# Hybrid decoder layer, down projection: activation loads for the next chunk kept behind a pair's sums on GpSimd's queue

## The chip, the cores and the metric

One core of one Trainium2 chip runs the whole layer in one launch. The metric is the device time of an execution in microseconds (us), and of several runs the median. TensorE is the engine of the matmuls (PE in the profile, PEld for its weight loads); VectorE is DVE, ScalarE is ACT, GpSimd is POOL, SyncE is SP. SyncE and GpSimd issue the DMA transfers.

## The reference, cut to what matters

The layer adds 16 meta tokens, runs two groups of heads and a projection, and ends with a SwiGLU feed-forward part on 512 tokens, a width of 2048 and an inner width of 5632:

```python
n2 = _rmsnorm(h, g_ffn[l])
h = h + (jax.nn.silu(n2 @ w_gate[l]) * (n2 @ w_up[l])) @ w_down[l]
return h[:, N_META:]
```

The change lies in the last product, `... @ w_down`, the down projection. All is float32.

## The kernel before, in words

Every float32 product is made of three products of a faster type: weights and activations are split into a rounded part and a remainder ("hi" and "lo"), and TensorE adds hi x hi, hi x lo and lo x hi. That is why matmuls stand in threes, lines 700 to 702 of `block_product`.

The feed-forward products use a scheme for 2 x 2 blocks with seven products in place of eight. For a pair of output tiles there are four weight blocks, "11", "12", "21" and "22", and seven products, each of a sum of weight blocks with a sum of activation blocks. `pair_product` (line 704) issues the seven products of a pair in PSUM banks x, y and z: x with block 0, z with 1, x with 2, z with 3, x with 4, y with 5, and x with 6. Between them ScalarE and VectorE take sums out: line 731 reads z, line 735 reads x after block 4, and only then may block 6 be added in x; line 738 reads y. With six inner tiles to a block, one block is 18 matmuls, and a pair 126.

**The weight side.** `prepare_pair` (line 627) makes the seven split weights of a pair, somewhat ahead of their use. `split_quad` (lines 604 to 609) copies a block to hi on ScalarE (line 607) and takes the remainder on VectorE (line 608). `add_quads` (line 611, the sum itself at line 614) makes t1 = "11" + "12" and t3 = "12" + "22"; lines 648 and 621 make t2. Each of the four weight blocks has one buffer, so the next pair's block is loaded by SyncE (`load_quad`, line 589) right after the last use of this pair's block: "12" after t3, "11" after its split, "22" after its split, "21" after its last sum. In the order that the scheduler chose, t3 of the next pair, which needs the new "22", stands on VectorE directly ahead of line 735 of the current pair.

**The activation side.** The 44 inner tiles are cut in four chunks, `CHUNKS = (4, 6, 6, 6)`, counted in pairs of tiles. The seven sums of activation blocks of each chunk lie in DRAM (`fd[c][s]`, chunk c, block s), hi and lo as two parts of 768 KB each (n = 6). `load_acts(c, s)` (line 919) brings one block back into SBUF with two DMAs on GpSimd's queue (line 930 in the profile). There are twelve places for blocks (`ring_place`), a chunk uses seven, so five blocks of the next chunk may come early, and two (5 and 6) can only come when the chunk's last pair has begun to free places.

**The loops.** Chunk 0 is run for four steps of four output tiles each (lines 982 to 997), chunks 1 to 3 for eight pairs of two output tiles each (line 998 on). After each pair, `down` (line 964) multiplies by the row scale (lines 967 and 974), and `add_down` (line 959) has GpSimd issue a DMA that adds the pair's sums to the output in DRAM, one for the odd tile (behind line 967), one for the even tile (behind the second product of line 974). In the last chunk the last pair is added on the chip instead (`so_far`, loaded at line 1010).

In the program's text the loads for the next chunk stand at the head of pairs 1 to 5 (blocks 0 to 4) and at the end of pair 7 (blocks 5 and 6). That isn't the order on the queue: a scheduler places each engine's instructions by when it believes them ready, and the loads depend on little, so they move ahead of the adds that wait for VectorE. In the built program the two parts of block 0 stand around the adds of the pair before, and all five blocks are issued over about two pairs.

Of the kernel before, what the change touches and what calls it, by code (L numbers as in the profile page):

```python
# [33 lines left out]
def hybrid_layer(ctx: ExitStack, tc: tile.TileContext, xT, w_in, w_out, w_gu, w_down, vecs, out):  # L34
# [10 lines left out]
    ve, sc, gp, pe = nc.vector, nc.scalar, nc.gpsimd, nc.tensor  # L45

    def open_pool(name, bufs=1, **kw):
        return tc.alloc_tile_pool(name=name, bufs=bufs, reuse_waits="tile", **kw)
# [251 lines left out]
    def two(t):  # L300
        return t.rearrange("p (a b) -> p a b", a=2)
# [402 lines left out]
    def pair_product(acts, c1, c2, fourth=None):  # L704

        i, cols = (used[0] - WIDE) // 7, c1.shape[-1]

        def bank(name):
            return xyz.tile([P, 512], F32, tag=name, name=f"{name}{i}")[:, :cols]

        def side(name):
            n = {"p1": 0, "p5": 1, "u2": 2}[name]
            if cols == T2 or not n:
                return sides[:, n * T2 : n * T2 + cols]
            return c2[:, 2 - n]

        y, z, x = bank("y"), bank("z"), bank("x")  # L720
        p1, p5, u2 = side("p1"), side("p5"), side("u2")
        if not i:
            block_product(y, acts[5], True)
        block_product(x, acts[0], True)
        sc.copy(p1, x)
        block_product(z, acts[1], True)
        sc.copy(p5, z)  # L727
        block_product(x, acts[2], False)
        sc.copy(u2, x)
        block_product(z, acts[3], False)  # L730
        ve.scalar_tensor_tensor(c2[:, 0], z, -1.0, u2, ALU.mult, ALU.subtract)
        if fourth:
            fourth()
        block_product(x, acts[4], False)
        ve.scalar_tensor_tensor(c2[:, 1], x, -1.0, p5, ALU.mult, ALU.subtract)  # L735
        if i:
            block_product(y, acts[5], True)
        ve.tensor_tensor(c1[:, 0], y, p1, ALU.add)
        block_product(x, acts[6], False)
        return x  # L740
# [9 lines left out]
    def slots(pool, dt, m, n, name, **kw):  # L750

        c = 2 * m * n * T2
        t = pool.tile([P, c + 64], dt, name=name, **kw)
        t = t[:, 4 : 4 + c].rearrange("p (s a k t) -> p s a k t", s=m, a=2, k=n)
        return [t[:, s] for s in range(m)]

    def slot(pool, dt, n, tag, name):
        return slots(pool, dt, 1, n, name, tag=tag)[0]

    def pad(pool, n):  # L760
        pool.tile([P, n // 4], F32, name=f"pad_{pool.name}")
# [19 lines left out]
    for i, j in enumerate(OUT_TILES):  # L781
# [32 lines left out]
        if i == KT - 1:  # L814
# [10 lines left out]
            rings, n_ring, ring = {}, [6], {}  # L825
# [3 lines left out]
            def new_places(i):  # L829
                p, m = groups[i]  # L830
                for n, t in enumerate(slots(rings_p[p], F32R, m, 6, f"ring{i}", tag=f"ring{i}")):
                    ring[i + n] = t

            def ring_place():
                n_ring[0] += 1
                return ring[(n_ring[0] - 1) % 12]
# [45 lines left out]
    fd = [[dram.tile([P, 2, n, T2], F32R, name=f"fd{c}_{s}") for s in range(7)] for c, n in enumerate(CHUNKS)]  # L882
# [33 lines left out]
            ve.scalar_tensor_tensor(odd[:, 4], odd[:, 3], -1.0, odd[:, 0], ALU.mult, ALU.subtract)  # L916
            store_acts(odd, 5, (5, 6, 1, 2, 3), f // 2)

    def load_acts(c, s):
        if c < len(CHUNKS):  # L920
            n = CHUNKS[c]
            if c:
                rings[c, s] = ring_place()[:, :, :n]
            elif s:
                rings[c, s] = slot(first, F32R, n, f"first{s}", f"first{s}")
            else:
                rings[c, s] = ring[0][:, :, :n]

            for part in range(2):
                gp.dma_start(rings[c, s][:, part], fd[c][s][:, part], max_dma_last_dim=3072)  # L930

    for f in range(FT):
        g1 = apool.tile([P, 2, T2], F32, tag="c1", name=f"g{f}")
        u1 = apool.tile([P, 2, T2], F32, tag="c2", name=f"u{f}")
        x = pair_product(acts, g1, u1, None if f else h_scale)
        if f < FT - 1:
            gate(f, g1, u1, x)
        if f == 2 * CHUNKS[0] + 1:
            load_acts(0, 0)
# [4 lines left out]
    with tc.high_priority(1 << 20):  # L944
        for s in range(1, 7):
            load_acts(0, s)
# [11 lines left out]
    def add_down(j, c):  # L958
        gp.dma_start(two(out[j]), c, accum_op=ALU.add)

    def part(c, n):
        return c[:, :, n * T2 : (n + 1) * T2]

    def down(c1, c2, acts, j, so_far):

        x = pair_product(acts, c1, c2)
        ve.tensor_tensor(c2, c2, r_h, ALU.mult)
        if so_far:
            ve.tensor_tensor(c2, c2, so_far[1], ALU.add)
            nc.sync.dma_start(two(out[2 * j + 1]), c2)  # L970
        else:
            add_down(2 * j + 1, c2)
        for k, src in enumerate((c1[:, 0], x)):
            ve.tensor_tensor(c1[:, k], src, r_h[:, k], ALU.mult)
            if so_far:
                ve.tensor_tensor(c1[:, k], c1[:, k], so_far[0][:, k], ALU.add)
        if so_far:
            nc.sync.dma_start(two(out[2 * j]), c1)
        else:
            add_down(2 * j, c1)  # L980

    for j in range(KT // 4):
        for s in range(2 * j - 2, 2 * j) if j else ():
            load_acts(1, s)
        c1, c2 = ((d, d_first)[j % 2][:, m : m + 2] for m in (0, 2))
        x = pair_product([rings[0, s] for s in range(7)], c1, c2)
        if j == KT // 4 - 1:
            first.release()
            rings_p[1] = open_pool("ring_a", side="right")
            for i in (1, 3, 4, 5):  # L990
                new_places(i)
            pad(rings_p[1], 160)
            load_acts(1, 6)
        sc.copy(c1[:, 1], x)
        for m, c in ((1, c2), (0, c1)):
            for n in range(2):
                add_down(4 * j + 2 * n + m, part(c, n))
    for c in range(1, len(CHUNKS)):
        for j in range(KT // 2):

            if 1 <= j <= 5:
                load_acts(c + 1, j - 1)
            c1, c2 = (two(d[:, j % 2 * 2 + m]) for m in range(2))
            so_far = None
            if c == len(CHUNKS) - 1 and j == KT // 2 - 1:

                hh = slots(rings_p[1], F32, 1, 6, "hh", tag="ring4")[0]
                so_far = [hh[:, :, n] for n in range(2)]
                for n in range(2):
                    gp.dma_start(so_far[n], two(out[2 * j + n]))  # L1010
            down(c1, c2, [rings[c, s] for s in range(7)], j, so_far)
            if j == KT // 2 - 1:
                for s in (5, 6):
                    load_acts(c + 1, s)
# [61 lines left out]
```

## Time and profile before

| | |
|---|---|
| median of 3 runs | 2087.51 us (2087.22 to 2088.33) |
| profiled execution | 2083.55 us |
| its span, first to last instruction | 2081.8 us |
| TensorE busy | 2056.5 us, 99% |
| VectorE, ScalarE, GpSimd busy | 1634.6, 1014.7, 389.2 us |
| mean granted TensorE clock | 0.997 |
| moved by DMA | 330.40 MB, mean 159 GB/s |

In the rows of the profile, "out<-in" names what an instruction writes and reads by the program's names, without buffer numbers; "idle before" is the time in which the engine had nothing to run just before the row, and what follows the arrow is what ended it. Matmuls overlap: one takes some 275 ns, but they follow each other by 0.11 to 0.12 us in the down projection. A DMA's "time to landing" runs from its issue to its completion.

The down projection runs from about 1645 us to the end. The adds to the output are `out_T<-d` (line 959), the blocks `ring<-fd` (line 930), the weights `b<-w_down` (line 589).

### The profile page before, as it was taken

How to read it: one execution, taken by the hardware profiler on the slowest of the kernel's cores; microseconds unless marked ns; L12 is line 12 of the kernel's file. 1: busy time of each engine (PE TensorE's matmuls, PEld its weight loads, DVE VectorE, ACT ScalarE, POOL GpSimd, SP SyncE). 2: the span in 40 equal slices, each digit the busy share in tenths (PEclk: the TensorE clock that was granted, in tenths of full speed). 3: DMA queues.
4: the chain of work that ended last, by engine and by line, in shares of the span. 5: the costliest groups of instructions: out<-in, count | busy, mean ns of one | idle time of the engine just before them, and what ended most of it. 6: DMA issues, size and time to landing. Idle time of an engine off the chain costs nothing.

```text
span 2081.8 us, 39149 instructions
## 1 busy us (share of the span) xinstructions
PE 2056.5 (99%) x16086; PEld 1982.3 (95%) x16086; DVE 1634.6 (79%) x2126; ACT 1014.7 (49%) x1516; POOL 389.2 (19%) x512
## 2 busy tenths in 40 slices
PE   8999999999999999999999999999999999999999
PEld 7999999999998888999999999999999999999999
DVE  8777767533336769999898899888988978888888
ACT  6666666322223434555555555555555554444443
POOL 4111111010103444111111011011111243131210
PEclk9999999999999999999999999999999999999999
DMA  5222222232235657546555465455455999697765
GB/s 175 81 72 80 73 82 72 85 97 92 92 103 169 183 178 237 160 138 194 162 152 170 146 182 150 146 172 168 137 173 158 284 336 340 148 332 163 206 149 109
DMA packets 144115, 330.40 MB, mean 159 GB/s; under 512 B 12400, under 2 KB 62064, under 8 KB 143936
## 3 DMA queue, kind: packets, MB, share of 16 engines
q1 hardware_dynamic: 67456, 212.50, 32.1%
q0 software_dynamic: 76480, 115.40, 21.7%
q8 instruction: 126, 2.06, 0.4%
q14 instruction: 53, 0.43, 0.1%
HBM read 260.74 MB, written 67.11 MB: 157 GB/s over the span
## 4 chain that ended last, share of the span: by engine, by line
PE 93%; DVE 4%; DMA 2%; ACT 1%; issue 1%; SPq 0%; DVEq 0%; ACTq 0%
PE x L700 11%; PE x L702 11%; PE x L701 11%; PE z L700 5%; PE z L701 5%; PE z L702 5%; PE y L700 3%; PE y L702 3%; PE y L701 3%; PE po L681 3%; PE po L679 3%; PE po L680 3%; PE pv L169 2%; PE pu L173 1%; PE pc L173 1%; PE pu L169 1%
## 5 line engine op out<-in xcount | busy, mean ns | idle before, releaser
L607 ACT CAST s<-t 128x1024 fp32r<-128x1024 f32 (+1 forms) x288 | 283.2, 983 | 371.6 <-PE z L702 165.2
L608 DVE TENSOR_TENSOR s<-t,s 128x1024 fp32r<-128x1024 f32 (+1 forms) x288 | 326.7, 1134 | 102.5 <-ACT s L607 100.5
L702 PE MATMUL x<-f,s 128*128 128x256 f32 x1408 | 387.3, 275 | 1.7 <-DVE s L608 1.7
L701 PE MATMUL x<-f,s 128*128 128x256 f32 x1408 | 387.3, 275 | 1.3 <-DVE f L184 1.3
L700 PE MATMUL x<-f,s 128*128 128x256 f32 x1408 | 387.2, 275 | 0.2 <-ACT f L183 0.2
L607 ACT CAST s<-b 128x1024 fp32r<-128x1024 f32 (+1 forms) x216 | 212.4, 983 | 159.3 <-PE x L702 140.3
L702 PEld LDWEIGHTS x<-f,s 128*128 128x128 f32 x1408 | 264.3, 188 | 1.9 <-DVE s L608 1.9
L701 PEld LDWEIGHTS x<-f,s 128*128 128x128 f32 x1408 | 264.3, 188 | 1.5 <-DVE f L184 1.5
L700 PEld LDWEIGHTS x<-f,s 128*128 128x128 f32 x1408 | 264.3, 188 | 0.5 <-ACT f L183 0.4
L608 DVE TENSOR_TENSOR s<-b,s 128x1024 fp32r<-128x1024 f32 (+1 forms) x216 | 246.3, 1140 | 2.4 <-ACT s L607 1.7
L138 DVE TENSOR_TENSOR wlo<-raw,whi 128x512 fp32r<-128x512 f32 (+1 forms) x198 | 142.3, 720 | 130.9 <-ACT whi L137 130.3
L892 POOL DMA_DIRECT2D fd<-s x147 | 103.8, 927 | 690.1 <-DVE s L184 673.6
L137 ACT CAST whi<-raw 128x512 fp32r<-128x512 f32 (+1 forms) x198 | 121.3, 614 | 185.4 <-PE pu L171 65.5
L700 PE MATMUL z<-f,s 128*128 128x256 f32 x704 | 193.8, 275 | 0.7 <-ACT sides L727 0.7
L701 PE MATMUL z<-f,s 128*128 128x256 f32 x704 | 193.6, 275 | 0.0
L702 PE MATMUL z<-f,s 128*128 128x256 f32 x704 | 193.6, 275 | 0.0
L614 DVE TENSOR_TENSOR t<-b,b 128x1024 f32<-128x1024 f32 (+1 forms) x144 | 165.8, 1152 | 17.3 <-DMA b<-w_down 12.7
L700 PE MATMUL x<-ring,s 128*128 128x256 f32 x608 | 169.3, 278 | 6.7 <-DVE d L735 5.7
L702 PE MATMUL x<-ring,s 128*128 128x256 f32 x608 | 168.9, 278 | 0.5 <-DVE s L608 0.5
L701 PE MATMUL x<-ring,s 128*128 128x256 f32 x608 | 168.7, 278 | 0.0
L700 PEld LDWEIGHTS z<-f,s 128*128 128x128 f32 x704 | 132.1, 188 | 0.9 <-ACT sides L727 0.9
L702 PEld LDWEIGHTS z<-f,s 128*128 128x128 f32 x704 | 132.1, 188 | 0.0
(351 smaller groups left out, 5602.4 us busy)
## 6 DMA issues: line engine op xcount, KB each, us to landing
b<-w_gu SPq DMA_DIRECT2D x176, 512.0 KB, 3.9
raw<-w_in SPq DMA_DIRECT2D x92, 512.0 KB, 3.3
fd<-s POOLq DMA_DIRECT2D x147, 256.0 KB, 5.4
b<-w_down SPq DMA_DIRECT2D x96, 384.0 KB, 4.1
ring<-fd POOLq DMA_DIRECT2D x42, 768.0 KB, 14.7
wide<-w_out SPq DMA_DIRECT2D x30, 512.0 KB, 3.5
out_T<-d POOLq DMA_DIRECT2D x54, 256.0 KB, 4.7
b<-w_down SPq DMA_DIRECT2D x16, 512.0 KB, 7.7
```

The source lines that it names most:

```text
L137: sc.copy(hi[:, :c], raw)
L138: ve.tensor_tensor(lo[:, :c], raw, hi[:, :c].bitcast(F32), ALU.subtract)
L169: pe.matmul(ps, wh, ah[:, a:b], start=k == 0, stop=False)
L607: sc.copy(hi, src)
L608: ve.tensor_tensor(lo, src, hi.bitcast(F32), ALU.subtract)
L614: ve.tensor_tensor(sums[name], a, b, ALU.add)
L679: pe.matmul(ps, hi[:, kk], ah, start=k == 0, stop=False)
L680: pe.matmul(ps, hi[:, kk], al, start=False, stop=False)
L700: pe.matmul(p, hi[:, kk], act[:, 0, k], start=start and j == k == 0, stop=False, skip_group_check=skip)
L701: pe.matmul(p, hi[:, kk], act[:, 1, k], start=False, stop=False, skip_group_check=skip)
L702: pe.matmul(p, lo[:, kk], act[:, 0, k], start=False, stop=k == n - 1, skip_group_check=skip)
L892: gp.dma_start(fd[c][s][:, :, k], t[:, :, i])
```

## The change

`load_acts` gets an argument. Where it is set, each of the two loads is tied behind the instruction that was recorded last on GpSimd before it, by an order of issue alone: no semaphore, no waiting for the earlier one to finish. It is set for the loads at the head of pairs 1 to 5 of a chunk and for those in chunk 0's loop, not for blocks 5 and 6 (line 1014), nor for block 6 of chunk 1 (line 993), nor for chunk 0's own blocks.

```diff
-    def load_acts(c, s):
+    def load_acts(c, s, in_order=False):
...
             for part in range(2):
-                gp.dma_start(rings[c, s][:, part], fd[c][s][:, part], max_dma_last_dim=3072)
+                load = gp.dma_start(rings[c, s][:, part], fd[c][s][:, part], max_dma_last_dim=3072)
+                if in_order:
+                    tc.keep_in_program_order(load)
...
     for j in range(KT // 4):
         for s in range(2 * j - 2, 2 * j) if j else ():
-            load_acts(1, s)
+            load_acts(1, s, True)
...
             if 1 <= j <= 5:
-                load_acts(c + 1, j - 1)
+                load_acts(c + 1, j - 1, True)
```

In the built program the other engines' order is unchanged. On GpSimd the order of the down projection becomes, with "adds" for the two adds of a pair (four in chunk 0's steps):

```
chunk 0:  adds, blocks 0 1 | adds, blocks 2 3 | adds, blocks 4 5 6 | adds
chunk 1:  adds, block 0 | adds, block 1 | adds, block 2 | adds, block 3 | adds, block 4 | adds | adds, blocks 5 6 | adds
chunk 2:  adds, block 0 | adds, block 1 | adds, block 2 | adds, block 3 | adds, block 4 | adds | adds, blocks 5 6 | adds
chunk 3:  adds, with the two loads of line 1010 around the first pair's
```

Before, blocks 5 and 6 had the same place; block 0's first part stood right behind them, and the rest of blocks 0 to 4 around the adds of the next two pairs.

## The prediction

> **What bounds the kernel now.** I read the page first (busy shares, DMA issues), then who TensorE waits for in the down projection, then the timelines and the chain of waits around those waits. All names are the program's; the line numbers are those of the kernel before.
>
> ```profile
> PE 2056.5 (99%) x16086; PEld 1982.3 (95%) x16086; DVE 1634.6 (79%) x2126; ACT 1014.7 (49%) x1516; POOL 389.2 (19%) x512
> b<-w_down SPq DMA_DIRECT2D x96, 384.0 KB, 4.1
> ring<-fd POOLq DMA_DIRECT2D x42, 768.0 KB, 14.7
> ```
>
> TensorE (PE) is busy 99% of the span, so the end moves only by what TensorE idles, or by time in which its matmuls run slower. The change touches only the loads in the last row (two parts to a block) and what stands beside them on GpSimd's queue. So the question is where TensorE waits because of them. In the chunks during which they move, TensorE's timeline shows five waits:
>
> ```profile
> 1751.00 0.36 PE L700 MATMUL x<-ring,s 128*128 128x256 f32 x1 [0.56 <-DVE d L735]
> 1766.74 0.36 PE L700 MATMUL x<-ring,s 128*128 128x256 f32 x1 [1.18 <-DVE d L735]
> 1840.24 0.36 PE L700 MATMUL x<-ring,s 128*128 128x256 f32 x1 [1.85 <-DVE d L735]
> 1871.66 0.36 PE L700 MATMUL x<-ring,s 128*128 128x256 f32 x1 [0.96 <-ACT s L607]
> 1959.73 0.36 PE L700 MATMUL x<-ring,s 128*128 128x256 f32 x1 [2.11 <-DVE d L735]
> ```
>
> VectorE is named in four of them, but the chain of waits shows what held VectorE up (start, length, what):
>
> ```profile
> 1831.17 7.53 DMA b<-w_down
> ...
> 1838.80 0.96 DVE t L614
> ...
> 1840.60 0.12 PE x L701
> ...
> 1841.18 0.21 PE x L700
> ...
> 1950.41 7.79 DMA b<-w_down
> ```
>
> A weight load issued at 1831.17 takes 7.53 us. The sum t3 of the next pair (L614) waits for it, L735 stands behind that sum on VectorE, and TensorE may not go on in bank x before L735. No ring block is late: a late weight block stops the pair, and it is late because ring loads are in flight. What an undisturbed pair does, and what the delay costs (timeline of VectorE, and the weight load's own rows, found by the time of issue):
>
> ```profile
> L589 SPq DMA_DIRECT2D b<-w_down x1: 327/327/327, 1816.9 to 1816.9; - x1
> DMA to landing us min/median/max: 3.0/3.0/3.0
> 1821.93 0.96 DVE L614 TENSOR_TENSOR t<-b,b 128x768 f32<-128x768 f32 x1
> 1838.80 0.96 DVE L614 TENSOR_TENSOR t<-b,b 128x768 f32<-128x768 f32 x1 [2.62 <-DMA b<-w_down]
> L589 SPq DMA_DIRECT2D b<-w_down x1: 327/327/327, 1743.2 to 1743.2; - x1
> DMA to landing us min/median/max: 6.2/6.2/6.2
> ```
>
> In the undisturbed pair the load (block "22" of the next pair) is issued at 1816.9, lands after 3.0, and the sum comes 5.0 us after the issue. At 7.53 VectorE waits 2.62 and TensorE 1.85; its first matmul after the wait takes 0.36 instead of 0.12, so 2.1 us are lost. At 7.79 it is 2.11 + 0.25 = 2.36, at 6.2 it is 0.56 + 0.25 = 0.81. All three fit one rule: **loss = T - 5.4 us**, where T is that load's time from issue to landing.
>
> There is a second cost. The windows' rows (length, busy time and count of PE, PEld, DVE, ACT, POOL, then granted clock, DMA share, GB/s):
>
> ```profile
> 806.78:810.19 3.41, 1.93 (x14) 1.54 (x13) 3.38 (x7) 2.60 (x6) 2.91 (x3) 1.00 1.11 380
> 810.19:813.60 3.41, 3.41 (x32) 3.41 (x31) 3.41 (x5) 2.83 (x6) 0.05 (x1) 1.00 1.12 377
> 1837.60:1841.01 3.41, 1.56 (x14) 1.39 (x14) 2.21 (x4) 0.83 (x1) 0.00 (x0) 1.00 1.14 405
> 1841.02:1844.43 3.41, 3.41 (x19) 3.41 (x18) 3.34 (x6) 0.11 (x1) 1.65 (x2) 0.50 1.15 407
> 1960.48:1963.90 3.42, 3.42 (x18) 3.42 (x17) 3.35 (x6) 0.09 (x1) 0.92 (x1) 0.50 1.08 363
> ```
>
> Behind the two longest waits the granted clock is 0.50 for 3.41 us: matmuls follow each other by 0.21 instead of 0.12, so some 16 of them cost 0.1 more each, 1.5 us. The half clock came right behind a stretch in which TensorE was busy 1.56 of 3.41 us (1837.60), and not behind one with 1.93 (806.78, with the row of 810.19 behind it). So the limit lies at an idle time between 1.48 and 1.85 us in such a stretch.
>
> All that these loads cost now: 0.81 + 1.43 + 2.10 + 1.21 + 2.36 for the five waits (idle time + 0.25) and 2 x 1.5 for the clock, 10.9 us. No reordering of them can gain more.
>
> **The change, part by part.** It adds and removes no instruction; in the built program the order of TensorE, VectorE, ScalarE and SyncE is the same. On GpSimd the loads no longer slide ahead of the pair sums. Now, GpSimd's timeline:
>
> ```profile
> 1810.70 0.86 POOL L959 DMA_DIRECT2D out_T<-d  x1 [9.91 <-DVE d L967]
> 1824.98 0.86 POOL L959 DMA_DIRECT2D out_T<-d  x1 [10.43 <-DVE d L967]
> 1827.97 0.86 POOL L959 DMA_DIRECT2D out_T<-d  x1 [2.13 <-DVE d L974]
> 1828.51 1.81 POOL L930 DMA_DIRECT2D ring<-fd  x2
> 1830.53 1.42 POOL L930 DMA_DIRECT2D ring<-fd  x2 [0.20 <-issue]
> 1832.57 0.70 POOL L930 DMA_DIRECT2D ring<-fd  x1 [0.62 <-PE x L702]
> ```
>
> A quiet pair lasts 14.28 us (1810.70 to 1824.98). At the end of a chunk four parts (blocks 5 and 6) go out right behind the adds of pair 6, and the ten parts of blocks 0 to 4 follow in a burst over the next two pairs. Changed, blocks 5 and 6 stay there (they aren't pinned), and blocks 0 to 4 go out two parts at a time behind the second add of pairs 0 to 4. They wait there for VectorE's last product (L974) with that add; nothing is behind them on the queue but the next pair's adds, 10 us later, and nobody needs the blocks before the next chunk. That happens for the blocks of chunks 2 and 3, so **ten pairs** get two parts each.
>
> *What goes.* The burst's waits: 1751.00, 1766.74 and 1871.66, 0.81 + 1.43 + 1.21 = **-3.45 us**. The one at 1871.66 names ScalarE; I count it because it lies in the same burst, and it would be 1.21 less gain if it has another cause. What is late next there is the same weight load, by the new loads (below).
>
> *What stays.* The waits at 1840.24 and 1959.73 with their half clocks. They come from the four parts of blocks 5 and 6, which keep their place. The first has one part less behind it (1832.57), but that went out after the weight load. I take 0.
>
> *What comes.* In each of the ten pairs two parts are issued 0.5 us behind the second add, so some 2.7 us ahead of the weight load (1828.51 against 1831.17). The trace has no pair with exactly two parts ahead. Its nearest rows, other than those above, are these: the first two of the four parts, and a weight load with two transfers of 256 KB ahead of it (near the end).
>
> ```profile
> L930 POOL DMA_DIRECT2D ring<-fd x2: 1062/1080/1097, 1828.5 to 1829.2; - x2
> DMA to landing us min/median/max: 7.1/8.5/9.9
> L589 SPq DMA_DIRECT2D b<-w_down x1: 328/328/328, 1967.7 to 1967.7; - x1
> DMA to landing us min/median/max: 4.9/4.9/4.9
> ```
>
> 0.5 MB ahead gives 4.9, four parts (3 MB) give 7.53 and 7.79, and a long backlog (1743.2) gives 6.2. A straight line between 0.5 and 3 MB would give 6.0 at 1.5 MB. But the second part landed at 1829.2 + 9.9 = 1839.1, after the weight load (1831.17 + 7.53 = 1838.70). The third and fourth stand behind it in GpSimd's queue, so they can have held the weight load up only a little, and leaving them out gains little. I take the row with the same place, less some 0.4: T = 7.2, with 6.2 and 7.8 as ends. Loss in each pair 7.2 - 5.4 = 1.77 (with the unrounded 5.43), in ten pairs **+17.7 us**; by the ends +7.7 and +23.7. TensorE then idles 1.52 us in a row, at the low edge of where the clock may fall, and only where that lies in one stretch: 0 for that, and a rival below.
>
> The Trainium skill, "DMA: Bandwidth & Descriptors", section "Queues, rings and completion order", says that each DMA engine takes turns between the queues that have work, a packet at a time. That speaks against this term, and gives a rival below.
>
> *The chunk before (four pairs of four tiles).* Chunk 1's blocks go out in groups of four, four and six parts behind three pairs' adds instead of earlier.
>
> ```profile
> 1707.66 1.11 POOL L959 DMA_DIRECT2D out_T<-d  x1 [0.78 <-DMA out_T<-d_first]
> L700 PE MATMUL y<-ring,s x144: 275/275/275, 1734.0 to 2075.4; 128*128 128x256 f32 x144
> ```
>
> The last six would go out right behind the add of 1707.66, and block 5 is first used at 1734.0. If the first of them lands after the page's 14.7 us, at 1723, and each further one 2.8 us later (9.9 less 7.1, above), block 5's second part, the fourth, is there by 1732: 0. With all of them landing one place later it would be 1 to 3 us too late, so 0 to +3; they cannot gain, since TensorE waits for none of them now.
>
> *Sum:* -3.45 + 17.7 = **+14.2 us**. The profiled execution took 2083.55 us for a span of 2081.8, the median of the runs is 2087.51, which is 3.96 longer; I add the difference to the median: **2101.7 us**. With the ends for T: 2091.8 to 2107.8.
>
> **Rivals.** (1) *The weight load doesn't wait behind two parts.* If DMA engines alternate between the two queues as soon as it arrives, it is delayed about as much as by the 0.5 MB row, T = 4.9, under 5.4. Then no new wait comes and the three old ones go: 2087.5 - 3.45 = 2084.1, not slower. It decides where T stays under 5.4 + 0.345. Against it: 6.2 at 1743.2, with a backlog, and 7.53 and 7.79. Chance 0.12. (The Trainium skill's turns, above, carried through, come to this.)
> (2) *Less of it*, T = 6.0 by the straight line: ten times 0.57 less 3.45, +2.2, 2089.7. For it speaks that half the bytes are queued, against it that the second part landed after the weight load. Chance 0.09.
> (3) *The half clock joins.* With T = 7.5 TensorE idles 1.8 us, close to 1.85, where the idle time lies in one stretch; in half of the ten pairs that adds 5 x 1.5 to 20.7 - 3.45: +25, 2112.5; in all ten 2120. For it: both rows of 7.53 and 7.79 had it. Against: neither 1.18 nor 0.96 had it. Chance 0.12.
> The Trainium skill, "TensorE: Matmul & The Clock Gate", section "Part 1: The HAM clock gate", puts the fall of the clock behind an idle window of about 3.4 us; by that, (3) would be out. The trace doesn't agree: it fell behind waits of 1.85 and 2.11 us.
> (4) *Chunk 1's blocks come late* by their later start: the 3 us from above on top of the forecast, 2104.7. Against it are the 2 us of room. Chance 0.04.
> That the change does nothing is out: the built order shows the loads moved.
>
> **How the numbers follow.** My forecast has the remaining 0.63, with 2092 to 2108 of its own. About 0.2% (4.2 us) is what a measurement of this kernel can tell from no change: 2083.3 to 2091.7 is "same". Slower: forecast 0.63, (3) 0.12, (4) 0.04, and 0.03 of (2), 0.82. Same: 0.06 of (2) and 0.07 of (1), 0.13. Faster: 0.05 of (1), should the waits at the chunks' ends shrink too. The range leaves out (1) below and the worse half of (3) above: 2087 to 2113.
>
> **What would show it.** In the profile after, GpSimd's timeline should show two ring parts behind the second add of pairs 0 to 4 of chunks 1 and 2. In those ten pairs the weight load issued some 3.2 us after that add should take about 7.2 us, L614 should wait 2.2 us for it, and TensorE's timeline should show ten waits of about 1.5 us before L700, all by L735; pair lengths 16.0 instead of 14.28. The two waits at the chunks' ends should be unchanged. I am wrong if the weight load lands within 5.4 us there, if the waits at the chunks' ends go too, or if PEclk falls in many slices from 1740 to 1950.

## The result and the profile after

| | before | after |
|---|---|---|
| median, us | 2087.36 (2084.28 to 2088.33, 4 runs) | 2107.23 (2104.07 to 2109.42, 4 runs) |
| profiled execution, us | 2083.55 | 2108.39 |
| its span, us | 2081.8 | 2106.7 |

The ratio of after to before is 1.0099, with a 95% interval of 1.0085 to 1.0112: the changed kernel is slower by 19.9 us. Forecast were 2101.7 us, and 2087 to 2113 as the range.

The page of the kernel after, two of its DMA rows:

```profile
b<-w_down SPq DMA_DIRECT2D x96, 384.0 KB, 4.1
ring<-fd POOLq DMA_DIRECT2D x42, 768.0 KB, 10.3
```

The ring loads themselves land sooner, 10.3 us instead of 14.7. The median of the weight loads is the same, 4.1, and hides what happens: of a pair's four weight loads that of block "22" is late, and VectorE waits for it, as the waits of the down projection show (1740 to 1990 us; who waits for whom, total, times, longest).

```profile
DVE t L614 <- DMA b<-w_down: 32.6, 12, 3.8
PE x L700 <- DVE d L735: 21.4, 10, 3.0
```

The same two rows of the kernel before:

```profile
DVE t L614 <- DMA b<-w_down: 12.1, 8, 2.9
PE x L700 <- DVE d L735: 5.7, 4, 2.1
```

TensorE's timeline after, the waits in those chunks one by one (start, length, idle time before it):

```profile
1758.04 0.36 PE L700 MATMUL x<-ring,s 128*128 128x256 f32 x1 [3.04 <-DVE d L735]
1775.28 0.36 PE L700 MATMUL x<-ring,s 128*128 128x256 f32 x1 [1.00 <-ACT s L607]
1792.58 0.36 PE L700 MATMUL x<-ring,s 128*128 128x256 f32 x1 [2.73 <-DVE d L735]
1809.64 0.36 PE L700 MATMUL x<-ring,s 128*128 128x256 f32 x1 [0.88 <-ACT s L607]
1825.69 0.35 PE L700 MATMUL x<-ring,s 128*128 128x256 f32 x1 [1.49 <-DVE d L735]
1856.39 0.35 PE L700 MATMUL x<-ring,s 128*128 128x256 f32 x1 [1.86 <-DVE d L735]
1886.97 0.36 PE L700 MATMUL x<-ring,s 128*128 128x256 f32 x1 [1.74 <-DVE d L735]
1903.85 0.36 PE L700 MATMUL x<-ring,s 128*128 128x256 f32 x1 [2.31 <-DVE d L735]
1920.71 0.35 PE L700 MATMUL x<-ring,s 128*128 128x256 f32 x1 [2.29 <-DVE d L735]
1937.26 0.36 PE L700 MATMUL x<-ring,s 128*128 128x256 f32 x1 [1.98 <-DVE d L735]
1953.84 0.36 PE L700 MATMUL x<-ring,s 128*128 128x256 f32 x1 [2.02 <-DVE d L735]
1986.27 0.35 PE L700 MATMUL x<-ring,s 128*128 128x256 f32 x1 [1.98 <-DVE d L735]
```

Ten of these are new; 1856.39 and 1986.27 are those of the chunks' ends. Two name ScalarE, but they too start 0.14 us behind the end of L735 (1775.14 and 1809.50 on VectorE's timeline), like the others. The first pair in detail, GpSimd's timeline and the weight load's own rows by time of issue (the adds of lines 959, 967 and 974 are lines 961, 969 and 976 of the changed kernel):

```profile
1744.86 0.85 POOL L961 DMA_DIRECT2D out_T<-d  x1 [2.11 <-DVE d L976]
1745.40 1.82 POOL L930 DMA_DIRECT2D ring<-fd  x2
```

```profile
L589 SPq DMA_DIRECT2D b<-w_down x1: 328/328/328, 1748.1 to 1748.1; - x1
DMA to landing us min/median/max: 8.4/8.4/8.4
```

Two ring parts go out behind the second add, the weight load 2.7 us later, and it takes 8.4 us. Over the ten pairs T (the same rows at each pair's load) is 8.4, 7.8, 8.0, 7.6, 6.7, 7.4, 7.5, 7.5, 7.2 and 7.2, on the mean 7.5. The half clock, in stretches of the windows view (length, busy time of PE first, granted clock third from the end; the stretch ahead of each half clock and the half clock itself, then one wait without):

```profile
1756.13:1759.54 3.41, 1.50 (x13) 1.53 (x14) 2.94 (x5) 0.00 (x0) 0.00 (x0) 1.00 0.32 87
1759.55:1762.96 3.41, 3.41 (x19) 3.41 (x18) 2.73 (x5) 0.83 (x1) 1.23 (x2) 0.50 0.92 233
1790.26:1793.67 3.41, 1.09 (x9) 1.12 (x10) 2.53 (x4) 0.46 (x1) 0.00 (x0) 1.00 0.28 70
1793.68:1797.09 3.41, 3.41 (x18) 3.41 (x17) 3.15 (x6) 0.42 (x1) 0.92 (x1) 0.50 0.88 237
1950.68:1954.09 3.41, 1.40 (x13) 1.23 (x12) 1.70 (x3) 0.83 (x1) 0.00 (x0) 1.00 0.43 164
1954.10:1957.51 3.41, 3.41 (x18) 3.41 (x18) 3.34 (x6) 0.00 (x0) 0.94 (x1) 0.50 0.80 221
...
1933.62:1937.02 3.40, 1.66 (x15) 1.46 (x13) 1.20 (x2) 1.33 (x2) 0.00 (x0) 1.00 0.64 239
1937.03:1940.44 3.41, 3.18 (x28) 3.21 (x28) 3.34 (x7) 0.00 (x0) 0.92 (x1) 1.00 0.59 159
```

It comes three times in the ten pairs, and no longer at the chunks' ends.

So that runs can be compared without the stages ahead, I use one more row: the first and last start of y's matmuls at L700, which span chunks 1 to 3. Before, the prediction's row gives 2075.4 - 1734.0 = 341.4 us. After:

```profile
L700 PE MATMUL y<-ring,s x144: 275/275/275, 1738.5 to 2100.3; 128*128 128x256 f32 x144
```

361.8 us, 20.4 more. By the rows above: the ten pairs' idle time is 19.5, with 0.25 each 22.0; three half clocks of 1.5, 4.5; the chunks' ends 4.3 instead of 4.5 + 3.0, -3.2; the old waits -3.45. That is +19.9.

### The profile page after: what moved, and what is told of

It reads as the page before. It is cut to its first block, busy times and chain, and to the rows that moved or that the text cites. A ratio compares the mean times of both kernels' runs of the same rounds, so it can differ in the third digit from the quotient of the medians.

```text
span 2106.7 us, 39149 instructions
## 1 busy us (share of the span) xinstructions
PE 2064.0 (98%) x16086; PEld 1988.2 (94%) x16086; DVE 1634.4 (78%) x2126; ACT 1013.3 (48%) x1516; POOL 388.6 (18%) x512
## 4 chain that ended last, share of the span: by engine, by line
PE 84%; DVE 7%; DMA 6%; ACT 1%; issue 1%; SPq 0%; DVEq 0%; ACTq 0%
PE x L700 9%; PE x L702 9%; PE x L701 9%; DMA b<-w_down 5%; PE z L700 5%; PE z L702 4%; PE z L701 4%; DVE s L608 3%; PE po L681 3%; PE po L679 3%; PE po L680 3%; PE y L702 2%; PE y L700 2%; PE y L701 2%; PE pv L169 2%; PE pu L173 1%
## 5 line engine op out<-in xcount | busy, mean ns | idle before, releaser
L608 DVE TENSOR_TENSOR s<-t,s 128x1024 fp32r<-128x1024 f32 (+1 forms) x288 | 326.7, 1134 | 105.0 <-ACT s L607 103.2
L700 PE MATMUL x<-f,s 128*128 128x256 f32 x1408 | 388.8, 276 | 0.2 <-ACT f L183 0.2
L700 PEld LDWEIGHTS x<-f,s 128*128 128x128 f32 x1408 | 265.6, 189 | 0.7 <-ACT f L183 0.4
L608 DVE TENSOR_TENSOR s<-b,s 128x1024 fp32r<-128x1024 f32 (+1 forms) x216 | 246.4, 1141 | 2.7 <-ACT s L607 2.1
L614 DVE TENSOR_TENSOR t<-b,b 128x1024 f32<-128x1024 f32 (+1 forms) x144 | 165.2, 1147 | 40.6 <-DMA b<-w_down 36.6
L700 PE MATMUL z<-f,s 128*128 128x256 f32 x704 | 193.8, 275 | 0.7 <-ACT sides L727 0.7
L700 PE MATMUL x<-ring,s 128*128 128x256 f32 x608 | 170.7, 281 | 23.3 <-DVE d L735 21.4
L700 PEld LDWEIGHTS x<-ring,s 128*128 128x128 f32 x608 | 116.4, 191 | 25.3 <-issue 18.5
L700 PEld LDWEIGHTS z<-f,s 128*128 128x128 f32 x704 | 132.2, 188 | 0.9 <-ACT sides L727 0.9
## 6 DMA issues: line engine op xcount, KB each, us to landing
ring<-fd POOLq DMA_DIRECT2D x42, 768.0 KB, 10.3
```

The lines of the kernel that those rows point to most:

```text
L608: ve.tensor_tensor(lo, src, hi.bitcast(F32), ALU.subtract)
L614: ve.tensor_tensor(sums[name], a, b, ALU.add)
L700: pe.matmul(p, hi[:, kk], act[:, 0, k], start=start and j == k == 0, stop=False, skip_group_check=skip)
```

## The experiments

The theory: two ring parts issued 2.7 us ahead of the load of block "22" make it late, t3 (L614) waits for it, and TensorE waits because L735 stands behind t3. Rivals: the loss comes from chunk 0; it comes from the amount of data and not from the place; the late transfers stop TensorE directly, whatever VectorE's order.

### Which part of the change costs

**Chunk 0's loads alone** keep their order (`load_acts(1, s, True)`; those at the head of pairs 1 to 5 float as before).

> Only the loads in chunk 0's four steps are pinned; in chunks 1 to 3 the loads slide as in the kernel before. Theory (the loss sits in the ten pairs where two parts go out 2.7 us ahead of the weight load of block 22): the time of before, with at most the one wait of 1.0 us more that the changed kernel showed at 1725 us, so 2087.4 to 2088.4 us, and the burst's waits of before are back. Rival A (chunk 1's blocks come late because chunk 0's steps hold them back, and the rest of the time follows from that): a good part of the 19.9 us stays, over 2095.

Measured: 2085.93 us, ratio to before 1.0006 (0.9996 to 1.0015).

```profile
L700 PE MATMUL y<-ring,s x144: 275/275/275, 1737.6 to 2078.2; 128*128 128x256 f32 x144
```

Chunks 1 to 3 take 340.6 us. Chunk 0's part of the change costs nothing that can be measured.

**The loads of chunks 1 to 3 alone:**

```diff
-            load_acts(1, s, True)
+            load_acts(1, s)
```

> The changed kernel with the order of issue kept only for the loads of chunks 1 to 3; those of chunk 0 (block loads for chunk 1) float as in the kernel before. My theory: all of the loss comes from the ten pairs of chunks 1 and 2, chunk 0 gave nothing when it was changed alone (1.0006): 2086 + 20 = 2106 us (2102 to 2108), waits behind L735 in the same ten pairs, T 7.2 to 8. Rival: the parts interact (chunk 0's order shifts what follows), and the time lies 5 us or more from that of the whole change.

Measured: 2109.98 us, ratio 1.0111 (1.0091 to 1.0131).

```profile
L700 PE MATMUL y<-ring,s x144: 275/275/275, 1737.8 to 2101.5; 128*128 128x256 f32 x144
```

363.7 us: the whole loss. The median lies 2 us above the end that I gave, but the interval of this ratio and that of the whole change overlap. So the two parts don't work on each other by more than the runs resolve.

### The place of the loads

**One part behind each add**, so that only one 768 KB part goes out 2.7 us ahead of the weight load, the other some 3 us earlier:

```diff
         add_down(2 * j + 1, c2)
+        if by_add:
+            by_add(0)
...
             add_down(2 * j, c1)
+        if by_add:
+            by_add(1)
...
+            by_add = (lambda n: load_acts(c + 1, j, True, (n,))) if j < 5 else None
```

> As changed, but in the ten pairs one part goes out behind each of the pair's two adds (some 5.7 and 2.7 us ahead of the weight load) in place of two behind the second. Theory (the weight load waits for what GpSimd's queue was given just ahead of it): about half of the bytes are still in the queue, so the weight load takes 5.9 to 6.9 us instead of 7.5, each pair loses 0.5 to 1.5 us, and the time is 2087.4 - 3.45 + 5 to 15 = 2089 to 2099, most likely 2094. Rival B (it is the volume: any pair that carries two parts loses the same, wherever they stand in it): 2107.

Measured: 2096.6 us, ratio 1.0057 (1.0041 to 1.0073).

```profile
L700 PE MATMUL y<-ring,s x144: 275/275/275, 1736.1 to 2089.3; 128*128 128x256 f32 x144
```

353.2 us; T is 6.1 to 7.7 in the ten pairs, on the mean 6.6 instead of 7.5. The loss over before falls from 20.4 to 11.8: it follows T.

**Both parts in the middle of the pair**, behind a small GpSimd copy that waits for line 731:

```diff
+            def middle():
+                if blocks and c + 1 < len(CHUNKS):
+                    gp.tensor_copy(mark[:, :1], c2[:, 0, :1])
+                    for s in blocks:
+                        load_acts(c + 1, s, True)
```

> As changed, but the two parts of the ten pairs are issued in the middle of the next pair: behind a GpSimd copy of one column that waits for VectorE's line 731, some 6.5 us behind the second add of the pair before and 3 us behind the issue of the weight load. Blocks 5 and 6 keep their place. Theory: the weight load of the pair lands in 3 to 3.5 us, the parts have landed before the next one, all ten waits go, the two at the chunks' ends stay: 2087.4 - 3.45 = 2084 us (2082 to 2086). Rival B (volume): the ten pairs still lose 2 us each, 2107; with a part of it on the other three weight loads of a pair, 2090 to 2100.

Measured: 2083.03 us, ratio 0.9994 (0.9985 to 1.0004). GpSimd's timeline (the copy is line 1010, the loads are line 932 in this version), then the next weight load "22" and two loads of other blocks by their times of issue:

```profile
1749.96 0.18 POOL L1010 COPY pad_h<-d 128x1 f32<-128x1 f32 x1 [5.85 <-DVE d L731]
1750.48 1.52 POOL L932 DMA_DIRECT2D ring<-fd  x2 [0.33 <-issue]
```

```profile
L589 SPq DMA_DIRECT2D b<-w_down x1: 328/328/328, 1760.5 to 1760.5; - x1
DMA to landing us min/median/max: 3.5/3.5/3.5
...
L589 SPq DMA_DIRECT2D b<-w_down x2: 328/328/328, 1752.3 to 1753.5; - x2
DMA to landing us min/median/max: 7.4/7.9/8.3
```

The same two parts, one pair at a time, now delay the loads of other blocks (7.4 and 8.3 us at 1752.3 and 1753.5), which have more room, and "22" takes 3.5 to 5.9. The ten waits are gone, save two of 0.33 and 0.34; the chunks' ends remain, with their half clocks. The bytes are the same, so it is the place and not the amount.

**Blocks 5 and 6 too in the middle of the chunk's last pair:**

```diff
-            blocks = [j - 1] if 1 <= j <= 5 else [5, 6] if j == KT // 2 - 1 and False else []
+            blocks = [j - 1] if 1 <= j <= 5 else [5, 6] if j == KT // 2 - 1 and True else []
...
-            if j == KT // 2 - 1:
-                for s in (5, 6):
-                    load_acts(c + 1, s)
```

> As mid, and blocks 5 and 6 are also issued in the middle of the chunk's last pair. Theory: the four parts miss that pair's weight load; they take some 13 us to land and so just reach into the next pair's weight load, which may take up to 4.5 us, under the 5.4 from which TensorE waits. All waits by these loads and their half clocks go: 2087.4 - 10.9 = 2076.5 us (2075 to 2080). Rival B (volume): four parts in one pair cost 2 to 4 us wherever they stand, so 2084 as mid or more; a second risk is that block 5 is late for the next chunk's first pair, which would show as TensorE waiting for the DMA of ring.

Measured: 2079.21 us, ratio 0.9971 (0.996 to 0.9983): faster than before. Both chunk ends go; what is left are two waits of 1.29 and 0.90 us in the next chunks' first pairs, into which the four parts reach, and one of 0.48.

### The order on VectorE

Here no load is moved. **t3 and L735 exchanged** in the changed kernel, by an order of issue alone (on VectorE these two are exchanged in each pair, and L608 with L976 beside them; the other engines' order is the same):

```diff
+        behind(i, name, ve.tensor_tensor(sums[name], a, b, ALU.add))
...
+    def behind(i, name, ins):
+        if i > FT + KT // 4 and name == "t3": tc.add_manual_dep(ins.ins, freed[-1].ins.name, NOSYNC, reason="t3")
...
+        freed.append(ve.scalar_tensor_tensor(c2[:, 1], x, -1.0, p5, ALU.mult, ALU.subtract))
```

> The changed kernel with two neighbouring VectorE instructions exchanged in each pair from the second pair of chunk 0 of the eleven-pair kind on (chunks 1 to 3): L735, which frees the sum x for TensorE, now stands ahead of the t3 sum L614 that waits for the late block 22. No load is moved. My theory: the load keeps its 7.5 us, the t3 sum still waits, but TensorE no longer does; next behind the t3 sum stands the low half of the following pair's first block (L608, s<-b), which TensorE needs one block product, 2.05 us, later than it needed L735. So of the twelve waits of 1.1 to 3.3 us (26.2 us in all) only what is over 2.05 us stays, 3.7 us, and no half clock: 2107.2 - 22.5 - 4.75 = 2080 us (2077 to 2085). Rival: TensorE waits because the transfers themselves are slow or because block 22 is needed at once, whatever the order on VectorE: the time stays within 4 us of 2107.

Measured: 2095.84 us, ratio 1.0055 (1.004 to 1.007): the rival is out, but of the 27 us that I expected only some 10 were gained (y's row is 351.8 against 361.8). The waits, 1740 to 1990:

```profile
DVE t L614 <- DMA b<-w_down: 28.2, 12, 3.2
PE x L700 <- ACT sides L725: 9.4, 12, 0.8
PE x L702 <- DVE s L608: 5.4, 8, 1.3
```

VectorE waits for the load nearly as long as before the exchange (32.6), and no wait of TensorE names L735 any more. In its place stand two others. L608, the low half of the next pair's first block, is the one that I had named, 5.4 us where I had given 3.7. L725 I had missed. VectorE's and ScalarE's timelines in one pair:

```profile
1750.96 0.96 DVE L614 TENSOR_TENSOR t<-b,b 128x768 f32<-128x768 f32 x1 [1.64 <-DMA b<-w_down]
1751.84 0.95 DVE L608 TENSOR_TENSOR s<-b,s 128x768 fp32r<-128x768 f32 x1
1754.84 0.95 DVE L648 TENSOR_TENSOR t<-t,b 128x768 f32<-128x768 f32 x1
```

```profile
1755.90 0.84 ACT L607 CAST s<-t 128x768 fp32r<-128x768 f32 x1 [4.13 <-DVE t L648]
1756.64 0.83 ACT L607 CAST s<-b 128x768 fp32r<-128x768 f32 x1
1757.38 0.36 ACT L725 COPY sides<-x 128x256 f32<-128x256 f32 x1
```

From t3's start VectorE works without a gap through what has queued behind it, two low halves, two row scales and L738 between the first and the last of these rows, and comes to L648 only at 1754.84. ScalarE waits for that with the cast of t2, and the copy of x (L725), which TensorE needs, stands two casts behind: x was complete at 1754.98, the copy began at 1757.38. The chain has a fixed length, so the wait is 0.78 to 0.80 in all twelve pairs.

**t3 behind L735 and behind the low halves of the next pair's first two splits** (t1 is the second), so that the work that TensorE needs is done ahead of the wait. The edit is against the run above; a split now also keeps its VectorE instruction, as a third item.

```diff
-        if i > FT + KT // 4 and name == "t3": tc.add_manual_dep(ins.ins, freed[-1].ins.name, NOSYNC, reason="t3")
+        if i > FT + KT // 4 and name == "t3": tc.add_manual_dep(ins.ins, split_w[-1][2].ins.name, NOSYNC, reason="t3")
```

> The changed kernel with the t3 sum put further back on VectorE, behind L735 and behind the low halves of the following pair's first two splits (L608). The loads stay where the change puts them. My theory: the loads still take 7.5 us, and nothing that TensorE needs within the next 4 us stands behind the wait: all twelve waits and their half clocks go, 2107.2 - 26.2 - 4.75 = 2076 us (2074 to 2080). Rival: block 12 of the next pair, whose buffer the t3 sum sets free, is loaded some 5 us later and the t1 sum then waits for it: waits of 1 to 3 us return in part of the pairs, 2085 to 2095 us.

Measured: 2073.82 us (2073.46 to 2075.62), ratio to before 0.9951 (0.9936 to 0.9966). This is the best version, some 31 us under the change as it was (0.9951 against 1.0099 of 2087). The waits of 1740 to 1990, the y row, and a load of "22" by its time of issue:

```profile
DVE t L614 <- DMA b<-w_down: 1.4, 2, 0.7
```

```profile
L700 PE MATMUL y<-ring,s x144: 274/275/276, 1737.3 to 2067.5; 128*128 128x256 f32 x144
```

```profile
L589 SPq DMA_DIRECT2D b<-w_down x1: 328/328/328, 1860.2 to 1860.2; - x1
DMA to landing us min/median/max: 7.7/7.7/7.7
```

The load is about as late as in the changed kernel (7.7 here; over the ten pairs 6.1 to 7.7, on the mean 7.2 against 7.5), and no wait of TensorE is left from 1740 to 1990. 330.2 us is 11.2 under before.

**The same on the kernel before** (the scheduler moved three adds on GpSimd's queue with it, each ahead of a ring load):

> The kernel before with the same exchange as in the run above (t3 sum behind L735 and two splits) and nothing else. My theory: its five waits of over 1 us behind block 22 go, three inside the chunks (3.45 us) and two at the chunk ends (4.6 us) with the half clocks behind them (up to 3.2 us): 2086 - 8 to 11 = 2075 to 2078 us, the same as the changed kernel with the exchange within 3 us, since with the exchange it no longer matters where the loads stand. Rival: the order of the loads costs something besides this one wait; then the two kernels with the exchange still lie 5 us or more apart.

Measured: 2078.79 us, ratio 0.9969 (0.9953 to 0.9984). **And on the version with all loads in the middle of a pair:**

> The version with all blocks of the next chunk loaded in the middle of a pair, and the t3 sum behind L735 and two splits. My theory: its two remaining waits at the chunk starts (1.53 and 1.14 us) and the small ones go, 2079.2 - 3 = 2076 us (2074 to 2079): the two remedies act on the same wait, so their gains do not add. Rival: they act on different losses and add up: 2079 - 9 = 2070 us.

Measured: 2080.61 us, ratio 0.9973 (0.996 to 0.9986). Both lie above the ranges that I gave, by 0.8 and 1.6 us. The same view of waits, of the kernel before so changed and then of the other:

```profile
DVE t L614 <- DMA b<-w_down: 11.5, 6, 2.7
```

```profile
DVE t L614 <- DMA b<-w_down: 21.1, 12, 2.7
```

With t3 put back, the kernel before and the changed kernel still lie 5.0 us apart in their medians, where I had given 3 as the most for the theory and 5 as the least for its rival. The intervals of the ratios just overlap (0.9953 to 0.9984, 0.9936 to 0.9966), and in the profiles y's rows differ by 3.2 (333.4 and 330.2). So the rival may hold in part; the waits speak for it, and how much it is worth stays open. L614 makes t1 as well as t3. In these two versions t1 waits, for block "12", whose load now goes out later because t3 sets its buffer free. In the middle version it meets the two ring parts there; t1 on VectorE's timeline:

```profile
1908.74 0.96 DVE L614 TENSOR_TENSOR t<-b,b 128x768 f32<-128x768 f32 x1 [2.17 <-DMA b<-w_down]
```

That is the rival I had set against the late t3 in the changed kernel. It is true where the loads go out in the middle of a pair, and not where they go out behind the adds: there the ring parts go out 1.7 us ahead of "22" and some 12 us ahead of "12", which takes 3.1 to 5.1 us. So the middle and the late t3 do not add: 2079.21 without and 2080.61 with the late t3, against medians of before of 2085.07 and 2086.35.

## Why the prediction was right

Right in direction and mechanism, and the time in its range, though +14.2 us were forecast and +19.9 measured. By its steps:

- **The place of the loads and whom they hit.** As forecast: two parts behind the second add, ten pairs, the weight load 2.7 us later, t3, L735, TensorE. The waits were to be about 1.5 us; they are 0.88 to 3.04. That VectorE's order is a link of the chain is shown by the exchange; that chunk 0 gives 0, by the first experiment (the profile after has one more wait of 0.77 us at 1725, ahead of chunk 1, but the run with chunk 0's loads alone has none there).
- **T.** 7.2 was forecast, 7.5 measured. The argument that the third and fourth parts matter little holds: the chunks' ends, with four parts, take 7.5 and 7.7 in the same profile. The two rivals with T = 4.9 and 6.0 are out. The Trainium skill, "DMA: Bandwidth & Descriptors", section "Queues, rings and completion order", has the engines take turns between queues; by the trace that does not keep a load of 384 KB from waiting behind parts issued 2.7 us earlier (7.5 us, where the prediction's quiet pair has 3.0).
- **Loss = T - 5.4.** This term was too small. In seven of the ten pairs the loss (idle + 0.25) is T - 5.0 to 5.2, in one T - 5.4. The rule was fitted to three of the five waits before. The wait at 1766.74, of 1.43 with the 0.25, has this load:

```profile
L589 SPq DMA_DIRECT2D b<-w_down x1: 328/328/328, 1758.8 to 1758.8; - x1
DMA to landing us min/median/max: 6.4/6.4/6.4
```

  That is T - 5.0, and so is the one at 1871.66 (1.21, T 6.2). The three that fit stand behind pairs in which TensorE had not waited, these two behind pairs in which t3 was late, as do most of the ten. The timelines show the link: in every pair the next load of "22" goes out 9.2 to 9.4 us behind t3's start, but TensorE begins block 6 2.02 us behind it in a quiet pair (1821.93 to 1823.95) and 1.44 us behind it after a wait (1885.53 to 1886.97). So a pair behind a delayed one has about half a us less room. At 1775.28 and 1809.64 the loss is T - 6.5: these come right behind the half clocks of 1759.55 and 1793.68. I read it so: TensorE has lost 1.5 us already, so it reaches the next wait later, and the half clock costs nothing more where the next pair waits anyway. The kernel before agrees, where behind the half clock of 1841.02 a load of 6.5 (issued at 1848.2) stopped TensorE not at all; no run separates it.
- **What comes** was thereby +22.0 + 4.5 and not +17.7. The half clock was put at 0 here and into a rival with five of ten pairs; it came in three.
- **What stays.** The waits at the chunks' ends stayed (1.86 and 1.98, forecast 1.85 and 2.11), but lost their half clocks, -3.2 where I took 0. The two errors in the half clock nearly cancel; the sum was 14.2 and is 19.9 mostly by the ten waits' size, 2.2 instead of 1.77 each, and to a smaller part by the half clocks (+1.3).
- **"No reordering of them can gain more than 10.9"**: the best version gains 11.2 between the same two matmuls, and 12.5 by its median (7 to 13 by the interval). Of the orders of the loads alone that were run the best, all in the middle, gained 5.9. What reached it was the order of one VectorE instruction, together with the change's order of the loads, and the prediction had no term for that.

## What to carry to other kernels

Before you reorder transfers, find which load has the least room and ask whether the room can be made larger: one sum that waited for a load stood ahead of an instruction that freed a bank of TensorE, and putting it further back made the same late load cost nothing. When you move a waiting instruction back, look at all that stands behind it on its engine, and at the in-order queues that wait for that (ScalarE's casts here), and at the loads that it sets off. An even spread of loads isn't better than a burst if each piece goes out just ahead of the load with the least room.

## What was not expected of the hardware

- Two parts of 768 KB issued 2.7 us ahead delay a 384 KB load on the other queue as much as four (mean 7.5 us; 7.5 and 7.7 at the chunks' ends). One part at that place and one 3 us earlier gives 6.6, and the prediction's load in a quiet pair 3.0.
- In the down projection the half clock follows a stretch of 3.41 us in which the profile has TensorE busy for 1.56 us or less (1.56 before; 1.50, 1.09 and 1.40 after), and not one with 1.66 of 3.40; the full-clock stretches of the other runs there lie on the same two sides. That share isn't the whole rule: near the launch, with other matmuls, a half clock (18.30 in the kernel before) follows a stretch with 1.75 of 3.41. The stretches lie on a fixed grid: the half clocks' starts, 1759.55, 1793.68 and 1954.10, are 10 and 47 times 3.413 us apart. So the same wait of some 2 us costs 1.5 us more or not by where it falls in the grid: 1.98 us before 1986.27 had none, 2.02 before 1953.84 had one. The Trainium skill, "TensorE: Matmul & The Clock Gate", section "Part 1: The HAM clock gate", puts the fall behind an idle window of about 3.4 us; here a stretch of that length that is busy for 1.5 us is enough.
